# Plain fp32 gate products and a new sharing-out of the splits in a recurrent mixer

## The chip, the cores and the metric

One Trainium2 chip, one of its cores. The metric is the device time of one execution of the whole kernel in microseconds. The kernel before has a median of 1291.49 us over 3 runs (1289.92 to 1292.58).

## What is computed

Two transformer blocks on 256 tokens of width 1024, all in fp32: block one is a recurrent mixer, a feed-forward part, an attention and a second feed-forward part; block two has two attentions and 32 routed experts. The change lies in the recurrent mixer at the very start, cut here to what matters:

```
u = x @ w_in + b_in                       # 1024 -> 2048, x is the normalized input
gate_branch, rec = u[:, :1024], u[:, 1024:]
rec = causal_depthwise_conv(rec, conv_w, conv_b)        # 4 taps along the tokens
gl[g] = rec (4 blocks of 256) @ gate_w[g] + gate_b[g]   # g = 0, 1; block diagonal
r_gate, i_gate = sigmoid(gl[0]), sigmoid(gl[1])
log_a = -8 * r_gate * softplus(-lam)
b = sqrt(-expm1(2 * log_a)) * (i_gate * rec)
h = associative_scan(h[t] = a[t] * h[t-1] + b[t])
y = (gelu(gate_branch) * h) @ w_out + b_out
```

## The kernel before, in words

**Weights and their splits.** All weights come through `Stream`: a list of units of up to 1 MB that SP loads in order into a ring of 17 buffers (`load`). Most products take fp32 operands apart into two parts in the reduced type fp32r, a rounded part H and a remainder L = raw - H, and TensorE forms H·H, H·L and L·H (`mm3`): three products where plain fp32 would have one. A unit is split in two halves by `pump`: a cast makes H (on ScalarE at L123, or on VectorE at L121 for the second halves of units 5 to 12), a subtraction makes L (on VectorE at L127, or on GpSimd at L125 for the first halves of units 1 to 10). `pump` runs at every `tick`, up to two units ahead.

**The units of the mixer**, in the order of TensorE's work: w0 and w1 (first two blocks of the recurrent half of w_in), w2 (gate weights of block 0), w3, w4 (gates 1), w5, w6 (gates 2), w7 (first block of the other half of w_in), w8 (gates 3), w9 to w11, then w12 to w15 (w_out). A gate unit is half as large as the others. Tiles are called by these numbers: w3H, w3L, and a number behind that is only a counter.

**A block of the recurrent half** (`rec_block`, lines 578 to 597): per feature half f, 24 products of 256 columns (`x_mm`), the bias on ScalarE (L589, into rc), the first tap of the convolution on VectorE (L591), three more taps there (L593), the rounding rH on ScalarE (L594) and the remainder rL on GpSimd (L595; on VectorE in block 3).

**A block of gates** (`gate_block`, from line 599): four outputs, each of two chunks of 128 features, so 2 x 3 = 6 products of 256 columns an output and 24 a block. Then two Tanh, an Exp and a Tanh on ScalarE per f, and two operations on VectorE into h.

**The recurrence** (L621 to L630): one Sqrt on ScalarE over all of T behind the last gates, four products (L626) and eight scans (L630) on VectorE; then `product` (L646 to L648) makes y's parts, which the output products (tile acc, from w12 on) read. The row b_out is added to the residual (tile xres) on GpSimd at L680; it is loaded at L260 into bo.

**Order.** The program is written in one stream, and a scheduler turns it into one queue per engine; each engine works its queue strictly in order, and a waiting instruction holds all behind it. SP's queue of loads is of the same kind: a load waits until its ring buffer is free.

Of the kernel before, what the change touches and what calls it, by code (L numbers as in the profile page):

```python
# [9 lines left out]
F32 = mybir.dt.float32  # L10
F32R = mybir.dt.float32r
AF = mybir.ActivationFunctionType
ALU = mybir.AluOpType
PSUM = bass.MemoryType.PSUM

P = 128
# [51 lines left out]
class Stream:  # L68
# [28 lines left out]
    def pump(self, upto=None):  # L97


        k, nc = self.k, self.k.nc  # L100
        end = 2 * self.done + SPLIT_AHEAD if upto is None else upto
        n = 0
        while self.pos < min(end, 2 * len(self.units)) and (upto is not None or n < self.most):
            i, half = divmod(self.pos, 2)
            self.pos += 1
            _, _, kc, cols, hl = self.units[i]
            if not hl:
                continue
            n += 1
            self.load(i + 1)  # L110
            if half == 0:
                H, L = k.big(F32R, f"w{i}H"), k.big(F32R, f"w{i}L")
                self.parts[i] = tuple(x[:, : kc * cols].rearrange("p (k n) -> p k n", k=kc) for x in (H, L))
            mid = (kc + 1) // 2
            s = slice(0, mid) if half == 0 else slice(mid, kc)
            raw, (H, L) = self.raws[i][:, s, :], (x[:, s, :] for x in self.parts[i])
            if self.units[i][0] in self.gated:
                g = self.gated[self.units[i][0]][:, None, :].to_broadcast(list(raw.shape))
                nc.vector.tensor_tensor(raw, raw, g, op=ALU.mult)
            if i in (5,6,7,8,9,10,11,12) and half == 1:  # L120
                nc.vector.tensor_copy(H, raw)  # L121
            else:
                nc.scalar.copy(H, raw)  # L123
            if i in (1,2,3,4,5,6,7,8,9,10) and half == 0:
                nc.gpsimd.tensor_tensor(L, raw, H.bitcast(F32), op=ALU.subtract)  # L125
            else:
                nc.vector.tensor_tensor(L, raw, H.bitcast(F32), op=ALU.subtract)  # L127
            if half == 1:
                del self.raws[i]
            if self.pos == self.end:  # L130
                self.ahead = RING
                self.load(self.done + self.ahead)
# [81 lines left out]
class Kern:  # L214
# [88 lines left out]

    def tok_mm(self, out, xT, cs, t, W, first, last):

# [8 lines left out]
def weight_units(A):  # L314
    U = []
# [10 lines left out]

    def gates(n):
        srcs = [(2 * g, 2 * g + 2, gw[g, n].rearrange("(k p) d -> p k d", p=P)) for g in range(2)]
        U.append((f"lg{n}", srcs, 4, 256, True))

    for n in range(4):
        if n == 0:
            srcs = [(4 * h, 4 * h + 4, rows(w, 512 * h, 512, D, 256)) for h in range(2)]
# [87 lines left out]
    for nh in range(2):  # L421
        for ih in range(2):
            srcs = [
                (2 * j + i, 2 * j + i + 1, rows(pair("down", nq - 1)[j], (2 * ih + i) * P, P, nh * 512, 512))
                for i in range(2) for j in range(2)
            ]
# [5 lines left out]
def two_blocks_kernel(ctx, tc, A, out, stop=None):  # L432
    nc = tc.nc
    k = Kern(ctx, tc, A)
    st = Stream(k, weight_units(A))
# [8 lines left out]
    xres = k.one.tile([P, 2, D], F32, tag="xres", name="xres")  # L444
    for t in range(2):
        for h in range(2):
            s = slice(512 * h, 512 * h + 512)
# [14 lines left out]

    def feat_mm(W, kc, f, mov):

        p = k.ps("pf")
        o = p[:, 0:256]
        (WH, WL), (mH, mL) = W, mov
        for i in range(kc):
            s = slice(f * P, (f + 1) * P)
            k.mm3(o, WH[:, i, s], WL[:, i, s], mH[:, i, :], mL[:, i, :], i == 0, i == kc - 1)  # L470
        return o
# [79 lines left out]
    for t in range(2):  # L551
        xn = k.t4(name="xn")
        for h in range(2):
            s = slice(512 * h, 512 * h + 512)
# [20 lines left out]
    recs = {}  # L575
# [3 lines left out]
    def rec_block(n):  # L579
        W = st.take(f"lr{n}")  # L580
        rc = k.t4(name="rc")[:, : 2 * 259].rearrange("p (f t) -> p f t", f=2)
        rec = k.t2(name="rec").rearrange("p (f t) -> p f t", f=2)
        rH = k.t2(F32R, name="rH").rearrange("p (f t) -> p f t", f=2)
        rL = k.t2(F32R, name="rL").rearrange("p (f t) -> p f t", f=2)
        nc.gpsimd.memset(rc[:, :, 0:3], 0.0)
        for f in range(2):
            c = 2 * n + f
            o = x_mm(W, f)
            nc.scalar.activation(rc[:, f, 3:259], o, AF.Identity, bias=k.pk("b_in", 8 + c))  # L589
            cw = lambda j: k.pk("conv_w", j * 8 + c)  # L590
            nc.vector.tensor_scalar(rec[:, f, :], rc[:, f, 0:256], cw(0), k.pk("conv_b", c), op0=ALU.mult, op1=ALU.add)  # L591
            for j in range(1, 4):
                nc.vector.scalar_tensor_tensor(rec[:, f, :], rc[:, f, j : j + 256], cw(j), rec[:, f, :], op0=ALU.mult, op1=ALU.add)  # L593
            nc.scalar.copy(rH[:, f, :], rec[:, f, :])  # L594
            (nc.vector if n in (3,) else nc.gpsimd).tensor_tensor(rL[:, f, :], rec[:, f, :], rH[:, f, :].bitcast(F32), op=ALU.subtract)  # L595
            tick()
        recs[n] = (rec, rH, rL)

    def gate_block(n):
        WH, WL = st.take(f"lg{n}")  # L600
        rec, rH, rL = recs.pop(n)
        T, ig = (x[:, n * 512 : (n + 1) * 512] for x in (Tall, hall))
        a = As[n // 2][:, (n % 2) * 512 : (n % 2 + 1) * 512]
        for f in range(2):
            c = 2 * n + f
            s = slice(f * 256, (f + 1) * 256)
            for g, dst in ((0, T), (1, ig)):
                W = (WH[:, 2 * g : 2 * g + 2, :], WL[:, 2 * g : 2 * g + 2, :])
                o = feat_mm(W, 2, f, (rH, rL))
                nc.scalar.activation(dst[:, s], o, AF.Tanh, bias=hb[:, 8 * g + c : 8 * g + c + 1], scale=0.5)  # L610
            nc.scalar.activation(a[:, s], T[:, s], AF.Exp, bias=m4[:, c : c + 1], scale=m4[:, c : c + 1])
            nc.scalar.activation(T[:, s], T[:, s], AF.Tanh, bias=sp2[:, c : c + 1], scale=sp2[:, c : c + 1])

        nc.vector.scalar_tensor_tensor(ig, ig, 1.0, rec.rearrange("p f t -> p (f t)"), op0=ALU.add, op1=ALU.mult)
        nc.vector.scalar_tensor_tensor(ig, a, 1.0, ig, op0=ALU.add, op1=ALU.mult)
        tick()
# [43 lines left out]
    W, os = st.take("lu0"), []  # L662
# [12 lines left out]
    bo = k.t4(name="bo")  # L675
    k.row("b_out", bo)
    for t in range(2):
        for nh in range(2):
            s = slice(nh * 512, (nh + 1) * 512)
            nc.gpsimd.tensor_tensor(xres[:, t, s], xres[:, t, s], bo[:, s], op=ALU.add)  # L680
    xT, rs, each = residual_norm(k.pk("ffn0", 0, 8))
    out_proj("lo", yT, each)
    if stop == "lru":
# [447 lines left out]
    for name in ("gm0", "gd0", "gm1", "gd1"):  # L1131
        g = gate[name] = k.t4(name="gate").rearrange("p (t n) -> p t n", t=2)
# [66 lines left out]
    lg = k.one.tile([P, 2, 40], F32, tag="lg", name="lg")  # L1199
# [95 lines left out]
    p = k.ps("pos")  # L1295
# [264 lines left out]
    for q in range(nq):  # L1560
        p = k.ps("gate")
# [11 lines left out]
        p = k.ps("up")  # L1573
# [104 lines left out]
```

## Time and profile before

| what | value |
|---|---|
| median of 3 runs | 1291.49 us |
| the profiled execution | 1291.26 us |
| its span, first to last instruction | 1289.6 us |
| TensorE busy | 1239.9 us (96%), 6311 products |
| VectorE busy | 733.3 us (57%) |
| ScalarE busy | 489.5 us (38%) |
| GpSimd busy | 109.3 us (8%), 114 instructions |
| HBM | 281 GB/s over the span |

The mixer fills about the first 112 us of the span. The sums and waits below are of the profiled execution. Matmuls are pipelined: a row of the timeline gives the start of a product and a duration that overlaps the next; the distance of two starts is what one costs in a stream. An engine's idle time stands in brackets with what ended it.

### The profile page before, as it was taken

Reading aid. Unit: us, or ns where it says so; the run is one execution under the profiler, and the core shown is the slowest. Engines: PE = TensorE matmul, PEld = TensorE weight load, DVE = VectorE, ACT = ScalarE, POOL = GpSimd, SP = SyncE. Lnnn points to the kernel's source line nnn. Section 1 sums busy time; section 2 is a strip of 40 time slices with the busy share of each in tenths; the row PEclk is TensorE's granted clock in tenths of the full one; section 3 lists DMA queues with packets and bytes.
Section 4 is the critical chain, followed back from the end, with each engine's and each line's share of the span. In section 5 each row is a group of like instructions: output and inputs, shape, how many; then the busy total and the mean of one; then the engine's idle time right before and its main releaser. Section 6 shows DMA issues by size and latency. Waiting matters only on the chain. (4 is left out here: it accounts for less than half of the span.)

```text
span 1289.6 us, 16077 instructions
## 1 busy us (share of the span) xinstructions
PE 1239.9 (96%) x6311; PEld 857.1 (66%) x6311; DVE 733.3 (57%) x1168; ACT 489.5 (38%) x847; POOL 109.3 (8%) x114
## 2 busy tenths in 40 slices
PE   5889999999999999999999999899999999999996
PEld 5888888998898888899777887543444434343332
DVE  6997668776544766978967685332233232222233
ACT  5575444456557653444656633310110101010111
POOL 6530000000122000010100000000000000000001
PEclk8999999999999999999999999999999999999999
DMA  8548767764434778765545466799999999999993
GB/s 279 194 137 320 260 237 266 272 205 153 142 130 156 272 242 288 238 234 188 170 161 164 151 240 266 279 423 421 419 422 421 421 422 422 420 421 421 422 418 145
DMA packets 121950, 362.97 MB, mean 281 GB/s; under 512 B 6288, under 2 KB 33680, under 8 KB 97808
## 3 DMA queue, kind: packets, MB, share of 16 engines
q1 hardware_dynamic: 121584, 361.39, 74.7%
q8 instruction: 51, 0.84, 0.3%
q10 hardware_dynamic: 288, 0.52, 0.1%
q14 instruction: 27, 0.22, 0.0%
HBM read 360.84 MB, written 1.05 MB: 281 GB/s over the span
## 5 line engine op out<-in xcount | busy, mean ns | idle before, releaser
L247 PE MATMUL up<-w,xs 128*64 128x512 f32 x512 | 131.5, 598 | 0.0
L247 PE MATMUL down<-w,hidT 128*64 128x512 f32 x512 | 126.8, 595 | 0.8 <-DVE hidT L1407 0.8
L247 PE MATMUL gate<-w,xs 128*64 128x512 f32 x512 | 123.0, 597 | 0.0
L1424 DVE SCALAR_TENSOR_TENSOR down<-down,wsl,g 128x512 f32<-128x512 f32 x30 | 22.8, 759 | 125.6 <-PE down L247 121.7
L247 PEld LDWEIGHTS down<-w,hidT 128*64 128x64 f32 x512 | 40.8, 137 | 71.9 <-issue 68.2
L1567 ACT ACTIVATE hid<-gate 128x512 f32<-128x512 f32 x16 | 9.6, 597 | 203.0 <-PE gate L247 203.0
L247 PEld LDWEIGHTS up<-w,xs 128*64 128x64 f32 x512 | 37.9, 136 | 67.8 <-issue 63.5
L247 PEld LDWEIGHTS gate<-w,xs 128*64 128x64 f32 x512 | 36.8, 137 | 64.8 <-issue 63.6
L709 DVE SCALAR_TENSOR_TENSOR adacc<-w,csil,adacc 128x512 f32<-128x512 f32 x84 | 65.1, 776 | 1.3
L1367 DVE TENSOR_SCALAR xs<-xs,geffP,modP 128x256 f32<-128x256 f32 x32 | 17.4, 543 | 73.5 <-PE xs L247 73.4
L1365 ACT ACTIVATE xs<-xs,modP,geffP 128x256 f32<-128x256 f32 x32 | 18.1, 565 | 97.7 <-DVE xs L1367 97.7
L518 DVE TENSOR_TENSOR xres<-comb,xres 128x512 f32<-128x512 f32 x64 | 40.3, 683 | 15.8 <-PE comb L247 15.8
L1425 ACT CAST oH<-down 128x512 fp32r<-128x512 f32 x30 | 17.6, 586 | 81.6 <-DVE down L1424 81.6
L1578 DVE TENSOR_TENSOR hid<-up,hid 128x512 f32<-128x512 f32 x16 | 11.1, 692 | 63.8 <-PE up L247 50.3
L777 DVE SCALAR_TENSOR_TENSOR sg<-tb,rs,sg 128x512 f32<-128x512 f32 (+1 forms) x24 | 16.9, 705 | 52.2 <-PE tb L247 52.1
L713 POOL TENSOR_TENSOR adL<-adacc,adH 128x512 fp32r<-128x512 f32 x12 | 20.0, 1667 | 311.0 <-ACT adH L712 311.0
L1478 POOL TENSOR_TENSOR out<-xres,fg 128x512 f32<-128x512 f32 x2 | 2.5, 1270 | 460.6 <-DVE xres L518 460.6
L266 ACT ACTIVATE junk<-xres 128x512 f32<-128x512 f32 x28 | 17.7, 631 | 53.6 <-DVE xres L518 50.9
L247 PEld LDWEIGHTS xs<-sel,xrH 128*128 128x128 f32 x128 | 21.8, 199 | 18.2 <-issue 16.9
L247 PE MATMUL xs<-sel,xrH 128*128 128x256 f32 x128 | 30.4, 306 | 2.6 <-DVE sel L1344 2.5
L763 ACT CAST hH<-hT 128x512 fp32r<-128x512 f32 (+1 forms) x24 | 13.2, 550 | 46.1 <-PE hT L760 46.1
L247 PE MATMUL comb<-oH,sT 128*128 128x512 f32 x62 | 26.5, 430 | 3.6 <-ACT oH L1425 3.6
(1322 smaller groups left out, 3422.8 us busy)
## 6 DMA issues: line engine op xcount, KB each, us to landing
w<-in_w_gate_dram SPq DMA_DIRECT2D x64, 1024.0 KB, 19.8
w<-in_w_up_dram SPq DMA_DIRECT2D x64, 1024.0 KB, 19.8
w<-in_w_down_dram SPq DMA_DIRECT2D x60, 1024.0 KB, 19.8
w<-in_ffn_w_in_dram SPq DMA_DIRECT2D x32, 1024.0 KB, 7.0
w<-in_w_ada_dram SPq DMA_DIRECT2D x24, 1024.0 KB, 5.3
w<-in_w_in_dram SPq DMA_DIRECT2D x20, 1024.0 KB, 5.0
w<-in_ffn_w_out_dram SPq DMA_DIRECT2D x16, 1024.0 KB, 6.1
w<-in_ffn_w_in_dram SPq DMA_DIRECT2D x16, 768.0 KB, 5.2
```

The lines of the kernel that those rows point to most:

```text
L247: self.nc.tensor.matmul(out, lhsT, rhs, start=start, stop=stop, skip_group_check=skip)
L266: self.nc.scalar.activation(junk[:, : src.shape[-1]], src, AF.Square, scale=scale, accum_out=acc)
L518: nc.vector.tensor_tensor(xres[:, t, s], p, xres[:, t, s], op=ALU.add)
L709: nc.vector.scalar_tensor_tensor(acc, raws[kh][:, i, :], c, acc, op0=ALU.mult, op1=ALU.add)
L713: nc.gpsimd.tensor_tensor(aL, acc, aH.bitcast(F32), op=ALU.subtract)
L763: nc.scalar.copy(hv, pv)
L777: nc.vector.scalar_tensor_tensor(h, p[:, :fw], rs[t], h, op0=ALU.mult, op1=ALU.mult)
L1365: nc.scalar.activation(o, pv, AF.Identity, scale=geffP[:, c : c + 1], bias=shP[:, c : c + 1])
L1367: nc.vector.tensor_scalar(o, pv, geffP[:, c : c + 1], shP[:, c : c + 1], op0=ALU.mult, op1=ALU.add)
L1424: nc.vector.scalar_tensor_tensor(p, p, ws, gates["g2"][:, s], op0=ALU.mult, op1=ALU.mult)
L1425: nc.scalar.copy(oH, p)
L1578: nc.vector.tensor_tensor(hv, hidden_order(q, p), hv, op=ALU.mult)
```

## The change

Four things, all within the mixer. The gate weights are no longer split (the units lg0 to lg3 are used as loaded), rec is no longer split, and a gate output is made by two plain fp32 products. All remaining castings of weights to H are on ScalarE, all remainders L on VectorE. The first tap of the convolution, with its bias, goes from VectorE to ScalarE. The addition of b_out goes from GpSimd to VectorE.

```diff
@@ Stream.pump
-            if i in (5,6,7,8,9,10,11,12) and half == 1:
-                nc.vector.tensor_copy(H, raw)
-            else:
-                nc.scalar.copy(H, raw)
-            if i in (1,2,3,4,5,6,7,8,9,10) and half == 0:
-                nc.gpsimd.tensor_tensor(L, raw, H.bitcast(F32), op=ALU.subtract)
-            else:
-                nc.vector.tensor_tensor(L, raw, H.bitcast(F32), op=ALU.subtract)
+            nc.scalar.copy(H, raw)
+            nc.vector.tensor_tensor(L, raw, H.bitcast(F32), op=ALU.subtract)
@@ weight_units, gates
-        U.append((f"lg{n}", srcs, 4, 256, True))
+        U.append((f"lg{n}", srcs, 4, 256, False))
@@ rec_block
-        rH = k.t2(F32R, name="rH").rearrange("p (f t) -> p f t", f=2)
-        rL = k.t2(F32R, name="rL").rearrange("p (f t) -> p f t", f=2)
-            nc.vector.tensor_scalar(rec[:, f, :], rc[:, f, 0:256], cw(0), k.pk("conv_b", c), op0=ALU.mult, op1=ALU.add)
+            nc.scalar.activation(rec[:, f, :], rc[:, f, 0:256], AF.Identity, scale=cw(0), bias=k.pk("conv_b", c))
-            nc.scalar.copy(rH[:, f, :], rec[:, f, :])
-            (nc.vector if n in (3,) else nc.gpsimd).tensor_tensor(rL[:, f, :], rec[:, f, :], rH[:, f, :].bitcast(F32), op=ALU.subtract)
@@ gate_block
-                W = (WH[:, 2 * g : 2 * g + 2, :], WL[:, 2 * g : 2 * g + 2, :])
-                o = feat_mm(W, 2, f, (rH, rL))
+                o = k.ps("pg")[:, 0:256]
+                for i in range(2):
+                    k.mm(o, W[:, 2 * g + i, f * P : (f + 1) * P], rec[:, i, :], i == 0, i == 1)
@@ the row b_out
-            nc.gpsimd.tensor_tensor(xres[:, t, s], xres[:, t, s], bo[:, s], op=ALU.add)
+            nc.vector.tensor_tensor(xres[:, t, s], xres[:, t, s], bo[:, s], op=ALU.add)
```

The line numbers move up by 6 to 10 in the changed kernel. What becomes of the queues is shown at three places.

TensorE at the gates of block 0, before: behind the last product of w1 (tile pf_357) come 24 products like these, six for each output (pf_392 is the first).

```order
L247 MATMUL pf_357<-xH_117,w1L_269 128x256
L247 MATMUL pf_392<-rH_233,w2H_306 128x256
L247 MATMUL pf_392<-rL_234,w2H_306 128x256
L247 MATMUL pf_392<-rH_233,w2L_307 128x256
L247 MATMUL pf_392<-rH_233,w2H_306 128x256
L247 MATMUL pf_392<-rL_234,w2H_306 128x256
L247 MATMUL pf_392<-rH_233,w2L_307 128x256
```

The same place in the changed kernel; w_36_223 is the gate weight as loaded, and pf_401 is the next block.

```order
L241 MATMUL pf_341<-xH_117,w1L_265 128x256
L241 MATMUL pg_374<-rec_232,w_36_223 128x256 x2
L241 MATMUL pg_378<-rec_232,w_36_223 128x256 x2
L241 MATMUL pg_384<-rec_232,w_36_223 128x256 x2
L241 MATMUL pg_388<-rec_232,w_36_223 128x256 x2
L241 MATMUL pf_401<-xH_117,w3H_335 128x256
```

24 products have become 8, of another kind, in the same place between the same neighbours.

VectorE from the remainder of w1 on, before (rec_232 is block 0, rec_315 block 1).

```order
L127 TENSOR_TENSOR w1L_269<-w_2_87,w1H_268 128x1024
L127 TENSOR_TENSOR w2L_307<-w_36_223,w2H_306 128x512
L591 TENSOR_SCALAR rec_232<-rc_231,pkt 128x256
L593 SCALAR_TENSOR_TENSOR rec_232<-rc_231,pkt,rec_232 128x256 x2
L591 TENSOR_SCALAR rec_232<-rc_231,pkt 128x256
L593 SCALAR_TENSOR_TENSOR rec_232<-rc_231,pkt,rec_232 128x256 x2
L127 TENSOR_TENSOR w3L_352<-w_37_226,w3H_351 128x1024
L593 SCALAR_TENSOR_TENSOR rec_232<-rc_231,pkt,rec_232 128x256
```

The same place in the changed kernel (rec_303 is block 1).

```order
L121 TENSOR_TENSOR w1L_265<-w_2_87,w1H_264 128x1024 x2
L121 TENSOR_TENSOR w3L_336<-w_37_226,w3H_335 128x1024
L585 SCALAR_TENSOR_TENSOR rec_232<-rc_231,pkt,rec_232 128x256
L121 TENSOR_TENSOR w3L_336<-w_37_226,w3H_335 128x1024
L585 SCALAR_TENSOR_TENSOR rec_232<-rc_231,pkt,rec_232 128x256 x4
L585 SCALAR_TENSOR_TENSOR rec_303<-rc_302,pkt,rec_303 128x256
L585 SCALAR_TENSOR_TENSOR rec_232<-rc_231,pkt,rec_232 128x256
```

Both halves of w1 and w3 now stand in this queue, one of block 0's three taps stands between the halves of w3, and the very last tap of block 0 stands behind the first of block 1.

VectorE at the end of the splits for the mixer, in the changed kernel; before, the rows of L670 were not in this queue.

```order
L121 TENSOR_TENSOR w12L_780<-w_86_645,w12H_779 128x1024 x2
L670 TENSOR_TENSOR xres<-xres,bo_906 128x512 x3
L606 SCALAR_TENSOR_TENSOR h_218<-h_218,rec_495 128x512
L670 TENSOR_TENSOR xres<-xres,bo_906 128x512
L607 SCALAR_TENSOR_TENSOR h_218<-a_216,h_218 128x512
L616 TENSOR_TENSOR h_218<-h_218,T_217 128x512 x2
L620 SCALAR_TENSOR_TENSOR h_218<-a_215,h_218 128x256 x4
```

The additions wait for the load of bo; three of them now stand ahead of the last block's first operation into h, the fourth between its two, and all ahead of the recurrence.

## Rows read from the trace of the kernel before

**Rows 1.** Page, whole run in 40 slices of 32 us: granted clock and DMA share, tenths.

```profile
PEclk8999999999999999999999999999999999999999
DMA  8548767764434778765545466799999999999993
```

**Rows 2.** TensorE's waits over the whole run: us in total, times, longest us.

```profile
PE pf L247 <- POOL w1L L125: 4.2, 1, 4.2
PE pf L247 <- DVE rL L595: 3.3, 1, 3.3
PE pf L247 <- DVE w4L L127: 3.0, 1, 3.0
PE pf L247 <- ACT rH L594: 1.4, 2, 0.9
PE pf L247 <- POOL rL L595: 1.0, 1, 1.0
```

**Rows 3.** Stretches: length, busy us (instructions) per engine, clock, DMA share, GB/s.

```profile
19.78:73.67 53.89, 41.06 (x289) 39.91 (x288) 50.99 (x59) 29.05 (x57) 32.52 (x25) 0.87 0.64 212
73.67:90.95 17.28, 17.28 (x147) 17.28 (x146) 17.14 (x26) 10.26 (x16) 5.19 (x3) 1.00 0.38 122
```

**Rows 4.** TensorE's timeline: start us, us, what, [idle before, releaser].

```profile
19.54 0.28 PE L247 MATMUL pf<-xL,w0H 128*128 128x256 f32 x1
19.66 0.28 PE L247 MATMUL pf<-xH,w0L 128*128 128x256 f32 x1
24.14 0.58 PE L247 MATMUL pf<-xH,w1L 128*128 128x256 f32 x1 [4.20 <-POOL w1L L125]
...
24.95 0.41 PE L247 MATMUL pf<-xH,w1L 128*128 128x256 f32 x1
25.16 0.41 PE L247 MATMUL pf<-xH,w1H 128*128 128x256 f32 x1
```

**Rows 5.** VectorE's timeline, the same columns.

```profile
17.96 1.23 DVE L127 TENSOR_TENSOR w1L<-w,w1H 128x1024 fp32r<-128x1024 f32 x1 [0.65 <-ACT w1H L123]
...
26.50 2.59 DVE L593 SCALAR_TENSOR_TENSOR rec<-rc,pkt,rec 128x256 f32<-128x256 f32 x1
...
47.82 0.48 DVE L593 SCALAR_TENSOR_TENSOR rec<-rc,pkt,rec 128x256 f32<-128x256 f32 x1
...
81.27 1.29 DVE L626 TENSOR_TENSOR h<-h,T 128x512 f32<-128x512 f32 x2
...
89.34 0.42 DVE L648 TENSOR_TENSOR yL<-gl,yH 128x256 fp32r<-128x256 f32 x1
```

**Rows 6.** GpSimd's timeline, the same columns.

```profile
25.46 3.35 POOL L125 TENSOR_TENSOR w3L<-w,w3H 128x1024 fp32r<-128x1024 f32 x1
...
70.99 7.87 POOL L680 TENSOR_TENSOR xres<-xres,bo 128x512 f32<-128x512 f32 x4 [2.80 <-DMA bo<-in_rows_dram]
```

**Rows 7.** TensorE's timeline at the end of the run, from three overlapping short stretches.

```profile
1279.98 0.70 PE L247 MATMUL comb<-o,sT 128*128 128x512 f32 x1 [0.84 <-DVE o L1481]
1280.51 1.45 PE L247 MATMUL comb<-o,sT 128*128 128x512 f32 x3
1280.94 1.02 PE L247 MATMUL comb<-o,sT 128*128 128x512 f32 x2
```

**Rows 8.** ScalarE's timeline, the same columns.

```profile
18.87 0.47 ACT L589 ACTIVATE rc<-pf,pkt 128x256 f32<-128x256 f32 x1
19.24 1.04 ACT L123 CAST w3H<-w 128x1024 fp32r<-128x1024 f32 x1
...
73.86 0.48 ACT L610 ACTIVATE h<-pf,hb 128x256 f32<-128x256 f32 x1 [0.22 <-PE pf L247]
...
76.77 1.92 ACT L621 ACTIVATE T<-T 128x2048 f32<-128x2048 f32 x1
```

**Rows 9.** Stretches late in the run, columns as in rows 3.

```profile
820.00:830.00 10.00, 10.00 (x56) 5.44 (x56) 2.31 (x5) 3.54 (x5) 0.00 (x0) 0.95 0.21 59
830.00:840.00 10.00, 10.00 (x56) 4.14 (x54) 2.61 (x10) 0.60 (x1) 0.00 (x0) 1.00 0.99 403
```

More of the change, by code (lines that the diff above doesn't have):

```diff
@@ L590, in rec_block @@
             cw = lambda j: k.pk("conv_w", j * 8 + c)
-            nc.vector.tensor_scalar(rec[:, f, :], rc[:, f, 0:256], cw(0), k.pk("conv_b", c), op0=ALU.mult, op1=ALU.add)
+            nc.scalar.activation(rec[:, f, :], rc[:, f, 0:256], AF.Identity, scale=cw(0), bias=k.pk("conv_b", c))
             for j in range(1, 4):
                 nc.vector.scalar_tensor_tensor(rec[:, f, :], rc[:, f, j : j + 256], cw(j), rec[:, f, :], op0=ALU.mult, op1=ALU.add)
-            nc.scalar.copy(rH[:, f, :], rec[:, f, :])
-            (nc.vector if n in (3,) else nc.gpsimd).tensor_tensor(rL[:, f, :], rec[:, f, :], rH[:, f, :].bitcast(F32), op=ALU.subtract)
             tick()
-        recs[n] = (rec, rH, rL)
+        recs[n] = rec
     def gate_block(n):
-        WH, WL = st.take(f"lg{n}")
-        rec, rH, rL = recs.pop(n)
+        W, rec = st.take(f"lg{n}"), recs.pop(n)
         T, ig = (x[:, n * 512 : (n + 1) * 512] for x in (Tall, hall))
```

## Prediction

> **What bounds the kernel now.** I began with the slices of the whole run [rows 1]. In the last fourteen or so the DMA engines are full (tenths of 9): expert weights stream there, and the end is their first load plus a fixed amount of transfer. Before that DMA has room, and TensorE's clock is full nearly everywhere. So two questions matter: where TensorE loses time before the stream of experts, and whether an earlier TensorE starts that stream earlier.
>
> TensorE's waits answer the first [rows 2]. The five lines that name the tile pf belong to the mixer and sum to 12.9 us: remainders of weights (w1L on GpSimd, w4L on VectorE) and the parts rH and rL of rec ahead of the gates. They all lie between 19.78 and 73.67 us, from the first product behind w0 [rows 4] to the end of the last gates. From 73.67 to 90.95, where the output products begin, TensorE is busy all the time, 17.28 of 17.28 us [rows 3], with the 144 products of w9 to w11, that is 0.12 us each, the distance of two starts in rows 4.
>
> So I take the first stretch apart. In its 53.89 us lie 190 products of w1 (46 that are left), w3, w5 and w7, and 96 of the gates. At 0.12 us these are 22.8 and 11.5 us. With waits of 12.8 us (the sum of the bracketed times) 6.8 us remain. They are the clock: its granted mean is 0.87 in this stretch [rows 3], and behind the 4.20 us wait products start 0.21 us apart instead of 0.12 [rows 4], TensorE at 1.2 GHz instead of 2.4. Waits and clock together: 19.6 us that hold no work.
>
> **Why the waits are there.** VectorE is busy 50.99 of the 53.89 us [rows 3], but much of that is not work. One tap of the convolution takes 0.48 us at 47.82 and 2.59 us at 26.50, where GpSimd is making w3L from 25.46 to 28.81 [rows 5, 6]. The tap ends when GpSimd does. The two engines hold each other up, and both make what TensorE waits for.
>
> **The change, part by part.**
>
> *Gates on TensorE.* 96 products go, 11.5 us. 32 plain fp32 products come; the trace shows each fp32 product as two records. At the end of the run records of 512 columns start 0.43 us apart (1280.51, 1280.94), the first one 0.53 ahead of the second [rows 7]. Half the columns at the steady rate: 0.215 a record, 0.43 a product. A block of eight is then 16 x 0.215 and 0.10 for the entry (0.53 - 0.43), 3.54 us; four blocks 14.2 us. That is 2.7 us more than the split gates cost. The lower end is 13.8 us without the entry; the upper end is a record of 256 columns at the price of one of 512, 64 x 0.43 = 27.5 us. I take the steady rate, because eight products in a row are nearest to the steady part of rows 7; with all records at the first one's rate (0.53 / 2 each) it would be 17.0.
>
> The Trainium skill speaks against this part: "FP8 and Floating Point Precision", section TensorE Precision Notes, says that true fp32 takes four passes through the array. An estimate by that rule, with the 0.12 us of an fp32r product [rows 4] for each pass, is 0.48 us a product and 15.4 us for all, and the sum below would give 1276.5 us instead of 1275.3.
>
> *Splits and rec off GpSimd.* In this part of the program GpSimd loses the ten remainders of weights, six of rec, and the four additions (7.87 us in all [rows 6]); behind its preparation at the start it has next to nothing. What it did for w2, w4, w6, w8 and rec vanishes. VectorE takes six remainders of 1.23 us [rows 5] and four additions of 0.65 (half of the 1.29 at 81.27), 10.0 us. It gives up eight casts, four remainders of half a unit (0.65 each), two of rec and eight first taps (0.48 each, 4.8 us with rec's); even with the casts at only 0.48 it gives up 11.2. Its own work does not grow, and what it loses to GpSimd goes.
>
> *ScalarE* takes six casts of 1.04 us and eight taps, which I price as the bias operation of the same shape, 0.47 [rows 8]: 10.0 us. It gives up six casts of half a unit and eight roundings of rec. It was busy 29.05 of 53.89 us [rows 3]. Cost nothing, while its queue keeps ahead of TensorE; the closest place is the next point.
>
> *Does each piece come in time?* With TensorE at 0.12 us from 19.78 on, the gates of block 0 are due at 25.3 (46 products). The last tap of block 0 now stands behind the first of block 1 on VectorE. That tap needs 24 products of w1, of which 22 follow 19.78: 22.4, plus 0.28 until the last is out [rows 4], then bias and first tap on ScalarE (0.47 each) and two taps on VectorE (0.48 each): 24.6. That leaves 0.7 us. The remainders of w1, now both on VectorE, are as close: at 17.96 the casts are done [rows 5], so the halves end by 19.2 and 20.4, and they are due at 19.8 and, 12 products later, 21.2. The following blocks have one or more groups of 5.8 us (48 products) between their rec and their gates.
>
> *The additions of b_out.* They wait for bo and hold the recurrence behind them on VectorE. Before, bo was there at 70.99 [rows 6], 2.7 us ahead of the end of the last gates. The recurrence cannot begin until ScalarE's Sqrt is done, 4.8 us behind the last gate output (73.86 to 78.69 [rows 8]). From there VectorE needs 8.5 us to the first remainder of y (81.27 to 89.76 [rows 5]): 13.3 us, against 17.3 of products that TensorE still has. So the additions are hidden as long as bo lands no later than some 6 us behind the gates; if it came later, each microsecond would stand ahead of the output products. On SP's queue bo now follows w14's load as before. No load is added.
>
> *Sum.* The stretch becomes 22.8 + 14.2 = 37.0 us instead of 53.9, 16.9 less. I leave 0.9 us for short waits that stay, the longer of the two for rH in rows 2. From there on the queues are the same rows in the same order. The profiled execution took 1291.26 us, 0.2 below the median of the runs: 1291.26 - 16.0 = **1275.3 us**.
>
> *Does it arrive at the end?* At 820 to 830 us DMA is nearly idle, 0.21, while TensorE is busy throughout, and from 830 on DMA is full [rows 9]. The ring is loaded and waits for buffers that TensorE must free, so the start of the full stream follows TensorE, and the end follows that.
>
> **The rivals.**
>
> *A. The fp32 products are dearer.* For it: no row shows 256 columns of plain fp32 in a chain. Against it: rows 7 run at a steady 0.43. Halfway to the upper end a record costs 0.32, 6.7 us more: 1282; at the upper end 13.8 more: 1289.
>
> *B. VectorE becomes the bound and some waits stay.* For it: in the 37.0 us it has 14 remainders (17.2 us), 24 taps (11.5) and six operations into h (3.9), 32.6 us in all. Against it: eight of the remainders are for w9 to w12, which TensorE needs only behind the stretch. A wait like the 3.3 us one with its third of the clock loss (6.8 / 3) costs 5.6 us: 1281 with one, 1286 with two.
>
> *C. The gain does not reach the end*, because the expert stream begins by something that does not move. Then 1291, no change. Against it: rows 9.
>
> *D. Slower: the gates wait for rec.* The first tap now goes TensorE, ScalarE, VectorE, TensorE, and ScalarE's place in it stands among the casts. If in all four blocks TensorE waited for rec, it would have to wait 4.0 us a block, clock included, to use up the 16.0. At 5.6 us each (as in B) the time would be 1275.3 + 22.4 = 1298. For it: only 0.7 us of room in block 0. Against it: in the other three the room is a whole group of products.
>
> **How the numbers follow.** What the runs can tell from no change is about 0.2%, 2.6 us. The forecast has 0.72, A 0.08, B 0.13, C 0.04 and D 0.03. Faster by more than 2.6 us are the forecast, B and nearly all of A: 0.92. Within it are C and the top of A: 0.05. Slower: 0.03. The range begins at 1272.7, the lower end of the gates without any wait left (16.9 + 0.4 from 1291.26) less the 1.3 us by which runs lie apart from the median. It ends at 1283.5, which takes in one wait of B and A to halfway; outside are C, D, two waits of B, the top of A and a little of the forecast, some 0.18.
>
> **What would show it.** In the profile of the changed kernel: TensorE without waits over 1 us between 20 us and the start of the output products, which moves from 90.95 to about 75; its clock at 1.00 there; fp32 records of pg 0.21 to 0.22 us apart; taps on VectorE near 0.48 us throughout; the full DMA stream beginning some 16 us earlier. I am wrong if waits for rec or for an L remain, if a record of pg costs over 0.3 us, or if the output products begin early and the end does not move.

## The result and the profile after

The change makes the kernel faster. Its median is 1276.07 us (4 runs, 1275.40 to 1277.22), beside 1292.03 us for the kernel before on the same chip (4 runs, 1289.92 to 1292.66): a ratio of 0.9879, with a 95% interval from 0.9867 to 0.9890. That is 16.0 us less; the forecast was 1275.3 us. The profiled execution is the slowest of the four, 1277.22 us with a span of 1275.6, so its rows hold about one microsecond that the median doesn't.

The stretches of [rows 3], as the kernel after has them, with the first group of products (those of w0) ahead of them. The columns are those of rows 3.

```profile
13.15:21.26 8.11, 8.00 (x50) 7.51 (x51) 7.36 (x17) 6.65 (x17) 6.77 (x18) 0.79 1.10 349
21.26:57.86 36.60, 36.60 (x257) 34.93 (x256) 31.08 (x47) 32.53 (x57) 1.05 (x3) 1.00 0.89 296
57.86:75.14 17.28, 17.28 (x146) 17.28 (x145) 14.65 (x29) 12.98 (x23) 0.00 (x0) 1.00 0.37 123
```

The second line answers to the first of rows 3: 36.60 us instead of 53.89, TensorE busy throughout, at a granted clock of 1.00 instead of 0.87. VectorE's busy time falls from 50.99 to 31.08 us although it took over about as much work as it gave up; GpSimd's falls from 32.52 to 1.05. The third line is the 17.28 us of before, unchanged.

TensorE's waits over the whole run, as in [rows 2]: of the lines that name pf one is left, and it lies at the start, ahead of the first product. The second line is new.

```profile
PE pf L241 <- ACT xH L295: 2.1, 1, 2.1
PE xs L241 <- PEq L1579: 1.6, 1, 1.6
```

TensorE's timeline: the gate products of blocks 0 and 1, and the first output product (start us, us, what).

```profile
26.78 3.62 PE L241 MATMUL pg<-rec,w 128*128 128x256 f32 x16
35.99 3.62 PE L241 MATMUL pg<-rec,w 128*128 128x256 f32 x16
...
75.13 0.40 PE L241 MATMUL acc<-w12H,yH 128*128 128x512 f32 x1
```

From one block's gates to the next are 9.21 us. The 48 products between take 5.76 at 0.12 us each, so 16 records take 3.45 us: 0.216 a record, 0.43 for a plain fp32 product. The output products start at 75.13 instead of 90.95.

VectorE's timeline, same columns; these answer to [rows 5].

```profile
24.26 3.37 DVE L585 SCALAR_TENSOR_TENSOR rec<-rc,pkt,rec 128x256 f32<-128x256 f32 x8
...
47.13 1.67 DVE L585 SCALAR_TENSOR_TENSOR rec<-rc,pkt,rec 128x256 f32<-128x256 f32 x4
...
56.81 1.89 DVE L670 TENSOR_TENSOR xres<-xres,bo 128x512 f32<-128x512 f32 x3
...
63.23 1.29 DVE L616 TENSOR_TENSOR h<-h,T 128x512 f32<-128x512 f32 x2 [2.45 <-ACT T L611]
```

Eight taps take 3.37 us together, 0.42 each; none takes over 0.5. The additions of b_out run at 56.81 without waiting for bo, and behind them VectorE still waits 2.45 us for ScalarE's square root, so they stand in nobody's way.

ScalarE's timeline: bias and first tap of the convolution; the tap costs 0.60 us, and the bias operation that it was priced by 0.46.

```profile
22.52 0.46 ACT L581 ACTIVATE rc<-pf,pkt 128x256 f32<-128x256 f32 x1
23.02 0.60 ACT L583 ACTIVATE rec<-rc,pkt 128x256 f32<-128x256 f32 x1
```

Late in the run, two stretches that lie 15 us ahead of those in [rows 9]: DMA goes from nearly idle to full as it did there.

```profile
805.00:815.00 10.00, 10.00 (x58) 5.12 (x58) 2.42 (x6) 3.73 (x7) 0.00 (x0) 1.00 0.25 78
815.00:825.00 10.00, 10.00 (x56) 4.16 (x54) 2.77 (x10) 0.53 (x1) 0.00 (x0) 1.00 1.01 426
```

The account of the profiled execution, 14.0 us less than before: from the first product behind w0 to the first output product it takes 53.87 us instead of 71.17 (-17.3). That first product comes 1.5 us later (21.26 instead of 19.78): ScalarE waited 1.2 us for the load of w0, so that TensorE began 0.7 us later (13.15 instead of 12.46), and the group of w0 ran at a granted clock of 0.79. Some 0.4 us go at the start of the expert part, and 1.4 at the branch of line 1579, where TensorE waits 1.6 us that it didn't wait before (last section).

### The profile page after: what moved, and what is told of

It is laid out like the page before. It is cut to its first block, busy times and chain, and to the rows that moved or that the text cites. A ratio compares the mean times of both kernels' runs of the same rounds, so it can differ in the third digit from the quotient of the medians.

```text
span 1275.6 us, 15951 instructions
## 1 busy us (share of the span) xinstructions
PE 1239.0 (97%) x6279; PEld 855.4 (67%) x6279; DVE 710.5 (56%) x1156; ACT 493.0 (39%) x847; POOL 74.5 (6%) x94
## 3 DMA queue, kind: packets, MB, share of 16 engines
HBM read 360.84 MB, written 1.05 MB: 284 GB/s over the span
## 5 line engine op out<-in xcount | busy, mean ns | idle before, releaser
L512 DVE TENSOR_TENSOR xres<-acc,xres 128x512 f32<-128x512 f32 x20 | 13.8, 691 | 28.6 <-PE acc L241 28.6
```

The lines of the kernel that those rows point to most:

```text
L512: nc.vector.tensor_tensor(xres[:, t, s], p, xres[:, t, s], op=ALU.add)
```

## The experiments

Eleven kernels, all compared with the kernel before on the same chip. The useful number beside the median is the **mixer length** in the profiled execution: from the first product behind w0 to the first output product. It is 71.17 us before and 53.87 after, and leaves out what differs at the start and behind it. Medians that lie less than about 2 us apart can't be told apart by these runs.

| kernel | median us | ratio to before, 95% | mixer length us |
|---|---|---|---|
| before | 1291.8 to 1292.3 | 1 | 71.17 |
| after | 1276.07 | 0.9879 (0.9867 to 0.9890) | 53.87 |
| e9 GpSimd's splits on VectorE, else before | 1282.41 | 0.9926 (0.9908 to 0.9944) | 60.37 |
| e2 fp32 gates alone, else before | 1283.01 | 0.9930 (0.9913 to 0.9946) | 59.70 |
| e1 after, gates split | 1276.32 | 0.9886 (0.9870 to 0.9903) | 55.44 |
| e4 after, six remainders on GpSimd | 1279.43 | 0.9912 (0.9896 to 0.9929) | 55.41 |
| e10 after, six needless GpSimd passes | 1285.33 | 0.9951 (0.9934 to 0.9967) | 63.25 |
| e11 after, six GpSimd fills | 1275.71 | 0.9873 (0.9857 to 0.9890) | 53.87 |
| e3 after, gates twice | 1289.07 | 0.9976 (0.9966 to 0.9986) | 67.68 |
| e8 after, gates of high parts | 1274.37 | 0.9861 (0.9845 to 0.9877) | 53.77 |
| e5 after, first tap on VectorE | 1276.35 | 0.9876 (0.9860 to 0.9893) | 53.86 |
| e12 after, tap and casts on VectorE | 1275.73 | 0.9878 (0.9861 to 0.9894) | 53.86 |
| e6 after, b_out on GpSimd | 1275.71 | 0.9875 (0.9858 to 0.9891) | 54.24 |

### GpSimd's splits given to VectorE, nothing else (e9)

```diff
-            if i in (1,2,3,4,5,6,7,8,9,10) and half == 0:
-                nc.gpsimd.tensor_tensor(L, raw, H.bitcast(F32), op=ALU.subtract)
-            else:
-                nc.vector.tensor_tensor(L, raw, H.bitcast(F32), op=ALU.subtract)
+            nc.vector.tensor_tensor(L, raw, H.bitcast(F32), op=ALU.subtract)
...
-            (nc.vector if n in (3,) else nc.gpsimd).tensor_tensor(rL[:, f, :], rec[:, f, :], rH[:, f, :].bitcast(F32), op=ALU.subtract)
+            nc.vector.tensor_tensor(rL[:, f, :], rec[:, f, :], rH[:, f, :].bitcast(F32), op=ALU.subtract)
```

> The kernel before with one edit: the ten remainders of weights and the six of rec that GpSimd made are made by VectorE (six of 1.22 us, four of 0.69, six of 0.41: 12.6 us more work); casts, first tap, split gates and b_out on GpSimd stay as they were. Theory (in the kernel before VectorE is held up by GpSimd's passes for some 20 of its 68 busy us between 19 and 89 us, more than it would take to make those remainders itself): faster than before, 1283 to 1289 us, with taps of 0.5 us until the additions of b_out. Rival (GpSimd takes work off VectorE, which is nearly full): slower than before, 1297 to 1304 us.

Measured: 1282.41 us, 9.4 less than before, a little better than the theory's range. An engine that was busy 95% of its stretch was given 16 more instructions and finished earlier. Two rows of VectorE's timeline, where GpSimd no longer works and where it makes the additions of b_out:

```profile
41.05 0.49 DVE L590 SCALAR_TENSOR_TENSOR rec<-rc,pkt,rec 128x256 f32<-128x256 f32 x1
...
51.08 1.51 DVE L590 SCALAR_TENSOR_TENSOR rec<-rc,pkt,rec 128x256 f32<-128x256 f32 x1
```

The same tap costs 0.49 us and 1.51. TensorE's longest wait in the mixer now lies just behind the additions, and the products after it start 0.21 us apart, at 1.2 GHz (granted clock 0.50 from 55.3 to 59 us):

```profile
55.31 0.58 PE L244 MATMUL pf<-rH,w8L 128*128 128x256 f32 x1 [2.79 <-DVE w8L L124]
...
57.79 0.41 PE L244 MATMUL pf<-rL,w8H 128*128 128x256 f32 x1
58.00 0.41 PE L244 MATMUL pf<-rH,w8H 128*128 128x256 f32 x1
```

### Plain fp32 gates, nothing else (e2)

The edit is the change's two pieces on the gates, in the kernel before.

```diff
-        U.append((f"lg{n}", srcs, 4, 256, True))
+        U.append((f"lg{n}", srcs, 4, 256, False))
...
-            nc.scalar.copy(rH[:, f, :], rec[:, f, :])
-            (nc.vector if n in (3,) else nc.gpsimd).tensor_tensor(rL[:, f, :], rec[:, f, :], rH[:, f, :].bitcast(F32), op=ALU.subtract)
...
-                o = feat_mm(W, 2, f, (rH, rL))
+                o = k.ps("pg")[:, 0:256]
+                for i in range(2):
+                    k.mm(o, W[:, 2 * g + i, f * P : (f + 1) * P], rec[:, i, :], i == 0, i == 1)
```

> The kernel before with only the gates changed to plain fp32 products; GpSimd keeps six first-half remainders and the additions of b_out, VectorE keeps its eight casts and the first tap. Theory (GpSimd's passes slow VectorE's, so what is gained goes with the share of them that is gone): GpSimd's share of the stretch falls from 32.5 us to about 20 us, VectorE's taps stay at over 1 us while GpSimd works, some waits and the lower clock stay: 1281 to 1288 us. Rival (unsplitting the gates is the gain, since it takes all the work that the gates waited for away): 1275 to 1278 us.

Measured: 1283.01 us, in the theory's range. It is 9.2 us less than before, about as much as e9 gives. GpSimd has ten passes less to make (four remainders of weights, six of rec), but VectorE, too, has six remainders and two casts less, and ScalarE fourteen casts; which of these carries the gain isn't parted by this run. Where GpSimd still makes a remainder, VectorE stands. Here GpSimd's row for w7L and that for w9L, and on VectorE a first tap and a rounding beside them, each with one that runs alone:

```profile
39.05 2.90 POOL L125 TENSOR_TENSOR w7L<-w,w7H 128x1024 fp32r<-128x1024 f32 x1 [1.27 <-ACT w7H L123]
...
46.01 2.57 POOL L125 TENSOR_TENSOR w9L<-w,w9H 128x1024 fp32r<-128x1024 f32 x1 [4.06 <-ACT w9H L123]
```
```profile
39.64 2.46 DVE L589 TENSOR_SCALAR rec<-rc,pkt 128x256 f32<-128x256 f32 x1
...
44.07 0.41 DVE L589 TENSOR_SCALAR rec<-rc,pkt 128x256 f32<-128x256 f32 x1
...
46.23 2.90 DVE L121 CAST w9H<-w 128x1024 fp32r<-128x1024 f32 x1
...
57.66 0.68 DVE L121 CAST w11H<-w 128x1024 fp32r<-128x1024 f32 x1
```

A tap that costs 0.41 us alone takes 2.46, a rounding of 0.68 takes 2.90, and both end up to 0.6 us behind GpSimd's pass. Both have one input tile.

### The change with split gates (e1)

```diff
-        U.append((f"lg{n}", srcs, 4, 256, False))
+        U.append((f"lg{n}", srcs, 4, 256, True))
...
+            nc.scalar.copy(rH[:, f, :], rec[:, f, :])
+            nc.vector.tensor_tensor(rL[:, f, :], rec[:, f, :], rH[:, f, :].bitcast(F32), op=ALU.subtract)
...
-                for i in range(2):
-                    k.mm(o, W[:, 2 * g + i, f * P : (f + 1) * P], rec[:, i, :], i == 0, i == 1)
+                o = feat_mm(W, 2, f, (rH, rL))
```

> The changed kernel with the gates in split fp32r products again, but with every split on ScalarE and VectorE and none on GpSimd. Theory (TensorE alone bounds the stretch from the second group to the last gate product, and VectorE and ScalarE have some 4 to 5 us of room in its 36.6 us): TensorE has 96 x 0.12 = 11.5 us instead of 13.8 us, but ScalarE gets 8 half casts and 8 roundings of rec (about 7 us) and VectorE as many remainders (about 7 us), which takes both past the stretch: 1278 to 1282 us, with new waits of the products for ScalarE or VectorE. Rival (the splits still hide, only the price of fp32 counts): about 2.3 us faster than the changed kernel, 1274 us. Rival (the gain came from unsplitting the gates, not from GpSimd's leaving): back near 1288 to 1292 us.

Measured: 1276.32 us, the same as the kernel after. All three expectations miss: the splits don't hide for nothing, and they don't cost much more than the cheaper products save. By the mixer length (55.44) they cost 1.6 us more than the 2.3 us that fp32r saves, too little for the medians to show. TensorE's waits have two lines that were not there, 1.6 us each:

```profile
PE acc L241 <- ACT yH L641: 1.6, 1, 1.6
PE pf L241 <- DVE w11L L121: 1.6, 1, 1.6
```

So fp32 gates are no part of the gain that couldn't be replaced: without them the median is 15.9 us below that of before, and the mixer 15.7 shorter instead of 17.3. What carries this lies in the other parts of the change. Of them GpSimd's splits given to VectorE are shown alone (e9); b_out, the casts and the tap share the rest.

### Six remainders back on GpSimd (e4)

```diff
-            nc.vector.tensor_tensor(L, raw, H.bitcast(F32), op=ALU.subtract)
+            (nc.gpsimd if 1 <= i <= 10 and half == 0 else nc.vector).tensor_tensor(L, raw, H.bitcast(F32), op=ALU.subtract)
```

> The changed kernel with one thing put back: GpSimd makes the six first-half remainders of the split weights 1, 3, 5, 7, 9 and 10 of the recurrent mixer. Theory (GpSimd's passes are what slowed VectorE and made the products wait): remainders of 3 us on GpSimd, taps of over 1 us beside them, waits of the products for w1L, w3L and rec, a lower clock behind them: 1280 to 1287 us. Rival (the stretch has the room, since VectorE has six passes less): no change, 1275 to 1277 us.

Measured: 1279.43 us, slower than after by 3.4, between the two ranges and nearer to the theory's. The mixer length grows by only 1.5 us. Of the waits that the theory named only the one for the first remainder is there:

```profile
PE pf L241 <- POOL w1L L121: 1.3, 1, 1.3
```

Beside a GpSimd pass VectorE's own remainder takes 3.45 us here instead of 1.22, 2.2 more; but each pass also spares VectorE 1.22 us. On balance VectorE's busy time over the mixer grows from 45.7 to 48.7 us, about 0.5 us a pass; in the next run nothing is spared. One could have concluded from this run alone that the two engines disturb each other little.

```profile
37.12 3.45 DVE L121 TENSOR_TENSOR w5L<-w,w5H 128x1024 fp32r<-128x1024 f32 x1
...
41.40 1.22 DVE L121 TENSOR_TENSOR w7L<-w,w7H 128x1024 fp32r<-128x1024 f32 x1
```

### What GpSimd's passes cost by themselves (e10, e11)

In both, six GpSimd passes stand behind VectorE's remainder of the first half, with a result that nobody reads. In e10 they read two tiles; in e11 they only write.

```diff
             nc.vector.tensor_tensor(L, raw, H.bitcast(F32), op=ALU.subtract)
+            if 1 <= i <= 10 and half == 0:
+                nc.gpsimd.tensor_tensor(raw, raw, H.bitcast(F32), op=ALU.subtract)
```
```diff
+                nc.gpsimd.memset(raw, 0.0)
```

> The changed kernel, in which GpSimd makes six more passes that nobody needs: behind VectorE's remainder of the first half of weights 1, 3, 5, 7, 9 and 10 it subtracts the same two tiles again, into the raw weight that is no longer read. No engine waits for these passes; only the refill of six weight buffers comes some 3 us later. Theory (GpSimd and VectorE exclude each other while both read two tiles): each of the six passes of about 2.4 us lengthens one VectorE instruction by about 2.2 us, 13 us of VectorE's time where it has 5.5 us of room in the stretch: slower than the changed kernel by 2 to 8 us, 1278 to 1284 us. Rival (what cost time before was waiting for GpSimd's results, not the two engines side by side): no change, 1275 to 1277 us.

> As the run with six unneeded GpSimd passes, but each fills the raw weight with zeros and reads nothing. Theory (the two engines exclude each other over reading): VectorE's instructions beside these passes keep their lengths (taps 0.48 us, remainders 1.22 us), no change, 1275 to 1277 us. Rival (any GpSimd pass on the same memory holds VectorE up, or the later refill of the buffers costs the time): slower by 2 us or more, 1278 to 1284 us.

Measured: e10 1285.33 us, 9.3 more than after, above the theory's range; e11 1275.71, no change. Six instructions whose results nobody needs take back more than half of the gain. GpSimd's and VectorE's timelines in e10:

```profile
22.88 3.22 POOL L123 TENSOR_TENSOR w<-w,w1H 128x1024 f32<-128x1024 f32 x1
26.06 2.53 POOL L123 TENSOR_TENSOR w<-w,w3H 128x1024 f32<-128x1024 f32 x1
...
42.69 2.55 POOL L123 TENSOR_TENSOR w<-w,w7H 128x1024 f32<-128x1024 f32 x1 [2.90 <-DVE w7L L121]
```
```profile
23.76 7.62 DVE L587 SCALAR_TENSOR_TENSOR rec<-rc,pkt,rec 128x256 f32<-128x256 f32 x8
...
42.94 3.39 DVE L121 TENSOR_TENSOR w7L<-w,w7H 128x1024 fp32r<-128x1024 f32 x1
```

The eight taps of 3.37 us take 7.62, and the remainder of 1.22 takes 3.39. In e11 the same places, with GpSimd's fills beside them:

```profile
23.65 1.84 POOL L123 MEMSET w<- 128x1024 f32 x2
```
```profile
23.42 3.37 DVE L587 SCALAR_TENSOR_TENSOR rec<-rc,pkt,rec 128x256 f32<-128x256 f32 x8
```

A fill of 0.92 us runs beside the taps, and they keep their 3.37 us. The later refill of the buffers isn't what costs the time either: in the mixer of e10 TensorE's waits name rec and no weight. So it isn't GpSimd at work that lengthens VectorE's instructions, but GpSimd reading. The Trainium skill states just this in "SBUF — State Buffer", section Who interferes with whom: a VectorE instruction with two inputs in SBUF, or in one of its two-port modes, shuts out a GpSimd instruction that reads SBUF and is shut out by it, for a whole instruction, while one that only writes doesn't disturb the two-input form. By that rule e10 is slow and e11 isn't, and the trace agrees: 7.62 against 3.37 us.

e10 loses more than expected. TensorE's timeline at the gates of block 0 and of block 3:

```profile
29.33 0.70 PE L243 MATMUL pg<-rec,w 128*128 128x256 f32 x2 [2.51 <-DVE rec L587]
30.52 4.98 PE L243 MATMUL pg<-rec,w 128*128 128x256 f32 x14 [0.49 <-DVE rec L587]
...
62.44 4.85 PE L243 MATMUL pg<-rec,w 128*128 128x256 f32 x14 [1.21 <-DVE rec L587]
```

TensorE waits for rec and then runs at the lower clock (granted mean 0.76 from 29 to 36 us): 14 records take 4.98 us, where 16 took 3.62. The expectation had no term for the clock. At block 0 this costs 5.2 us, with longer VectorE instructions ahead of it and no wait of VectorE for GpSimd. At block 3 it costs 4.2; there one of VectorE's remainders also waited for a GpSimd pass to end, which the expectation had left out, and what that wait alone costs isn't parted from the rest:

```profile
54.29 1.22 DVE L121 TENSOR_TENSOR w10L<-w,w10H 128x1024 fp32r<-128x1024 f32 x1 [2.26 <-POOL w L123]
```

### Where TensorE stands (e3, e8)

e3 computes each gate sum twice; e8 is e1 with one product of the high parts in place of three.

```diff
-                for i in range(2):
-                    k.mm(o, W[:, 2 * g + i, f * P : (f + 1) * P], rec[:, i, :], i == 0, i == 1)
+                for i in range(4):
+                    k.mm(o, W[:, 2 * g + i % 2, f * P : (f + 1) * P], rec[:, i % 2, :], i % 2 == 0, i % 2 == 1)
```
```diff
-                o = feat_mm(W, 2, f, (rH, rL))
+                o = k.ps("pg")[:, 0:256]
+                for i in range(2):
+                    k.mm(o, W[0][:, i, f * P : (f + 1) * P], rH[:, i, :], i == 0, i == 1)
```

> The changed kernel with each gate sum computed twice (the second group overwrites the first). Theory (TensorE bounds the stretch, and a plain fp32 product costs two records of 0.216 us): 64 more records, 13.8 us more, all of it on the path: 1289 to 1291 us, with the output products starting at 89 us. Rival (VectorE or ScalarE bounds the stretch beside TensorE, and the gates fill time that would be waiting): under 10 us more, 1284 us or less.

> The changed kernel with the gates computed from the rounded high parts of weights and rec alone, one fp32r product in place of one fp32 product, the low terms left out; the splits of the gates' operands are made on ScalarE and VectorE all the same. TensorE's gates cost 32 x 0.12 = 3.8 us instead of 13.8. Theory (with so much less on TensorE, VectorE and ScalarE bound the stretch, with 38 us and 39 us of work): the same as the kernel with split gates on these engines, 1275 to 1278 us, with more waits of TensorE. Rival (TensorE still bounds it): 10 us less than the changed kernel, 1266 us.

Measured: e3 1289.07 us, and a mixer length of 67.68, 13.81 us more: 64 records of 0.216 us are 13.8, so all of it is on the path. e8 1274.37 us, 0.6 us below the theory's range and far from the rival's 1266. Against e1, which has the same splits, 64 products or 7.7 us are gone from TensorE, and the mixer length falls by 1.7. The stretches of e8:

```profile
21.52:58.00 36.48, 33.60 (x262) 31.66 (x261) 33.44 (x60) 34.46 (x71) 0.86 (x5) 1.00 0.88 290
58.00:75.29 17.29, 13.46 (x108) 12.85 (x107) 16.05 (x24) 12.99 (x18) 0.00 (x0) 1.00 0.49 146
```

ScalarE is busy 34.46 of 36.48 us and VectorE 16.05 of the 17.29 behind it, and TensorE's waits name VectorE's w11L (1.8 us) and ScalarE's yH (1.6). In the kernel after, TensorE sets the length of the mixer; with split gates the other two are as close, and less work on TensorE alone brings next to nothing.

### The small moves (e5, e12, e6)

e5 puts the first tap back on VectorE, e12 that and the second-half casts of w5, w7, w9 to w12, e6 the additions of b_out on GpSimd.

```diff
-            nc.scalar.activation(rec[:, f, :], rc[:, f, 0:256], AF.Identity, scale=cw(0), bias=k.pk("conv_b", c))
+            nc.vector.tensor_scalar(rec[:, f, :], rc[:, f, 0:256], cw(0), k.pk("conv_b", c), op0=ALU.mult, op1=ALU.add)
```
```diff
-            nc.scalar.copy(H, raw)
+            if i in (5,6,7,8,9,10,11,12) and half == 1:
+                nc.vector.tensor_copy(H, raw)
+            else:
+                nc.scalar.copy(H, raw)
```
```diff
-            nc.vector.tensor_tensor(xres[:, t, s], xres[:, t, s], bo[:, s], op=ALU.add)
+            nc.gpsimd.tensor_tensor(xres[:, t, s], xres[:, t, s], bo[:, s], op=ALU.add)
```

> The changed kernel with the first tap of the convolution back on VectorE. VectorE gets eight passes of about 0.41 us, 3.3 us more in a stretch where it is busy 31.1 of 36.6 us; ScalarE gives up eight of 0.60 us. Theory (TensorE bounds the stretch, both engines have room): no change, within 1 us of 1276 us. Rival (ScalarE's 32.5 us of 36.6 are what the stretch runs to): faster by 1 to 3 us. Rival (VectorE is at its limit): slower by 1 to 3 us.

> The changed kernel with the first tap and the roundings of the second halves of weights 5, 7, 9, 10, 11 and 12 back on VectorE; GpSimd stays idle. VectorE gets 3.3 + 6 x 0.69 = 7.4 us, more than the 5.5 us it has free in the stretch; ScalarE gives up about 11 us. Theory (TensorE, VectorE and ScalarE are all within some 5 us of one another): slower by 1 to 4 us, 1277 to 1280 us, with waits of the products for VectorE's remainders. Rival (TensorE alone bounds it, roundings and tap moved for nothing): no change, within 1 us of 1276 us.

> The changed kernel with the four additions of b_out back on GpSimd. Theory (a GpSimd pass holds VectorE up for about its own length, but these four come when the last gates run and VectorE has over 5 us of room): VectorE gives up 2.6 us and loses up to about 6 us to GpSimd's passes around 57 to 65 us, hidden or nearly: 1275 to 1278 us. Rival (any GpSimd pass beside VectorE reaches TensorE): 1279 to 1283 us.

Measured: 1276.35, 1275.73 and 1275.71 us, none to be told from the kernel after. For e12 the theory had named 1 to 4 us more, and missed. Its first stretch:

```profile
20.91:57.50 36.59, 36.59 (x257) 34.92 (x255) 36.08 (x59) 22.91 (x43) 2.65 (x7) 1.00 0.92 302
```

VectorE is busy 36.08 of 36.59 us and TensorE waits for nothing. The extra work came to 5.0 us and not 7.4: instructions that follow each other start closer together than one takes (first taps 0.33 us ahead of the next instruction where one lasts 0.41, casts 0.60 where one lasts 0.69). With fp32 gates, then, the moves of casts and tap to ScalarE bring nothing. With split gates it is otherwise: e1 differs from e9 by casts, tap and b_out, and these are worth 6.1 us there (4.9 by the mixer length). Which of the three carries that was not tried; in e9 the wait of 2.79 us and the lower clock stand just behind GpSimd's additions of b_out, which points at that one without showing it.

## Why the prediction was right

*The stretch and its sum.* Predicted: 37.0 us instead of 53.9, no waits over 1 us, clock at 1.00. Measured 36.60, no wait, 1.00. That GpSimd's passes alone can bring back both waits and lower clock is shown by e10, for 9.4 of the 17.3 us by which the mixer became shorter. That all of the 19.6 us had this one cause isn't shown: e9, in which GpSimd keeps b_out and VectorE its casts and tap, shortens the mixer by 10.8.

*fp32 products.* Predicted 3.54 us a block, 14.2 in all. Measured 3.45 and 13.8: the steady rate was right (0.215 predicted, 0.216 measured), and the 0.10 us for entering a block wasn't there. By the page "FP8 and Floating Point Precision" of the Trainium skill, section TensorE Precision Notes, four passes were estimated at 0.48 us a product; the trace has 0.43, so the measurement decides against that estimate, by 1.6 us over 32 products. The estimate took 0.12 us for a pass; the rows show two records of 0.216 us a product and no passes, so that whether the count or the price of a pass is off they don't tell. Rival A is out. (Its upper end lies 13.3 us above the sum's 14.2, not 13.8; the 1289 us stay.)

*GpSimd holding VectorE up.* Predicted from one tap of 2.59 us beside one of 0.48. e9 shows it: VectorE takes the passes over and is done sooner. e10 and e11 tie it to GpSimd's reading. In the prediction's sum the gates appear only with their price of 2.7 us; e2 shows that unsplitting them alone is worth 9.2 us, since it ends ten of GpSimd's passes and some of the other engines' work with them. The two ways overlap: 9.4 (e9) and 9.2 (e2) would be 18.6 together, and the whole change brings 16.0.

*VectorE's work.* The prediction gave it 32.6 us in the stretch (rival B), of which the remainders for w9 to w12 could come later; measured 31.08, with the remainders for w9 to w12 all inside. Rival B didn't come about.

*ScalarE.* Additions of 10.0 us were to be hidden. They are, but the tap was priced at 0.47 us and takes 0.60, 1.0 us more over eight. That VectorE now idles 1.7 us for a cast at two places (w5L, w12L) costs nothing, since TensorE doesn't wait.

*Rec in time for block 0.* Predicted with 0.7 us of room; the gates start at 26.78, behind the 46 products from 21.26 on, without a wait, but the room was next to nothing. In the kernel after, ScalarE's first tap of block 1; and on VectorE the next tap of block 1, with the last tap of block 0 behind it:

```profile
24.67 0.60 ACT L583 ACTIVATE rec<-rc,pkt 128x256 f32<-128x256 f32 x1
```
```profile
25.84 0.87 DVE L585 SCALAR_TENSOR_TENSOR rec<-rc,pkt,rec 128x256 f32<-128x256 f32 x2
```

The last tap ends at 26.71, 0.07 us ahead of the gates. The prediction let VectorE begin block 1 as soon as ScalarE was done, which was at 25.27; VectorE came to it at 25.84, since half of w3L and four taps of block 0 stood ahead in its queue, a term that the working left out. That TensorE didn't wait here is luck rather than a result of the working. In e10 it is there that TensorE waits first, 2.51 us. Rival D, in which all four blocks wait, didn't come about; in the other three rec is done 4 to 6 us ahead of the gates.

*b_out.* Hidden, as predicted; e6 shows that it doesn't matter which engine adds.

*The end.* The start of the full stream follows TensorE [rows 9]: the same step from idle to full lies 15 us earlier. Rival C is out, and e3 shows the reverse: time added to the mixer arrives at the end. But the end is not the stream's first load plus a fixed transfer, as the prediction has it. The last loads of expert weights on SP's queue, and TensorE's first product behind the branch, each before and after:

```profile
1240.72 23.66 SPq L93 DMA_DIRECT2D w<-in_w_down_dram  x16
```
```profile
1224.49 24.18 SPq L93 DMA_DIRECT2D w<-in_w_down_dram  x16
```
```profile
917.00 0.47 PE L247 MATMUL xs<-sel,xrH 128*128 128x256 f32 x2
```
```profile
902.96 0.48 PE L241 MATMUL xs<-sel,xrH 128*128 128x256 f32 x2 [1.58 <-PEq L1579]
```

The last loads begin 16.2 us earlier, the end of the span only 14.0 (1275.6 instead of 1289.6), and that is TensorE's lead at the branch (14.04). From there to the end it is 372.6 to 372.8 us in all thirteen profiles, and no wait of TensorE names a load. So the end follows TensorE through the stream of experts too: the mixer's gain arrives, and so does what TensorE loses later, such as the wait at the branch.

*The sum.* The 0.9 us left for short waits, and the 0.4 for entering blocks, weren't used, so that the mixer gained 17.3 us and not 16.0. In the profiled execution 1.5 us went at the start, 0.4 at the start of the expert part and 1.4 at the branch, none of them foreseen. In the median 0.8 us are left between 1275.3 and 1276.07, less than the runs can tell; that the two lie so close is in part luck, since errors of both signs meet in it.

## What to carry to other kernels

Before giving an engine's surplus to GpSimd, look in the timeline at what VectorE's instructions last beside it: where a 0.4 us tap takes 2.5, as here, the helper can cost more than it takes over, and a nearly full VectorE can be done sooner by doing the work itself (e9). Busy time that contains such holds isn't work, so compare the shortest and the longest instance of one shape. And when two edits each remove part of one cause, price the sum by the bottleneck behind it (here TensorE's 36.6 us), not by adding their gains.

## What the runs showed of the hardware

- VectorE instructions with one input tile are held by a GpSimd pass too: a tap by scalars 2.46 us instead of 0.41, a rounding 2.90 instead of 0.68 (e2). The page "SBUF — State Buffer" of the Trainium skill, section Who interferes with whom, names these two operations among those that can enter a two-port mode and then contend with GpSimd; the trace shows the time, not the mode.
- It goes both ways: beside VectorE's remainders GpSimd's tiny preparation steps take 1.1 to 1.4 us; the same steps take 0.2 to 0.3 in e10, where VectorE stands still (21.33 and 21.55 us). The kernel after, GpSimd's timeline:

```profile
17.88 1.36 POOL L562 TENSOR_SCALAR s<-pkt 128x8 f32<-128x8 f32 x1
19.21 1.15 POOL L563 TENSOR_SCALAR a<-a 128x8 f32<-128x8 f32 x1
20.44 0.20 POOL L564 TENSOR_TENSOR a<-a,s 128x8 f32<-128x8 f32 x1
```

- At the branch of the expert part (line 1579 after) TensorE's sequencer takes 1.5 to 1.7 us in six of the thirteen profiles, 0.2 in one and nothing in six, among them the one of the kernel before. The code there is the same in all; what decides it stays open. In the profile of the kernel after it costs 1.4 us of TensorE's lead: 15.46 us at the products ahead of the branch, 14.04 behind it.
